# Every product of a transformer trunk layer in plain fp32 on four 32-column tiles, in place of three fp32r products of high and low parts

## The chip, the cores and the metric

The kernel runs on one core of a Trainium2 chip. The metric is the device time of one execution in microseconds, as the median of several runs. TensorE multiplies: a stationary operand of up to 128 columns is loaded into its array and a moving operand of up to 512 columns is streamed past it, into PSUM. VectorE (DVE) and ScalarE (ACT) work on SBUF and PSUM, GpSimd (POOL) does little here, and SyncE (SP) issues nearly all DMAs.

## The reference, cut to what matters

One layer of a diffusion backbone, applied to 128 context tokens and 256 latent tokens (384 together), with model width 2048. All inputs and outputs are fp32.

```python
h = rms_norm(x, n1) * (1 + sc1) + sh1
q, k, v, u = project_in(h, w_in, q_g, k_g)             # 2048 -> 4096
attn = attend(q, k, v)                                 # 16 heads of 64
na, fn = attn @ w_na_proj, fourier_mix(u) @ w_fnet_proj      # 1024 -> 2048 each
g_na, g_fn = split(sigmoid(h @ w_gate))                # 2048 -> 4096
x = x + g1 * ((g_na * na + g_fn * fn) @ w_o)           # 2048 -> 2048
h2 = rms_norm(x, n2) * (1 + sc2) + sh2
a, g = split(h2 @ w_gate_up)                           # 2048 -> 11264
x = x + g2 * ((silu(g) * a) @ w_down)                  # 5632 -> 2048
```

The six shifts, scales and gates come from two conditioning vectors through `w_mod` (2048 to 12288).

## The kernel before, in words

**A product.** TensorE takes operands of a type fp32r, a rounded fp32. To keep the precision of fp32 the kernel writes each operand as a high part H (rounded to fp32r) and a low part L (the rest, rounded too), and adds three products, H·H, H·L and L·H, into the same PSUM bank. `split` (L154 to L156) makes the parts: ScalarE casts to H, VectorE subtracts. `mm3` (L158 to L161) issues the three matmuls, one line each, so L159, L160 and L161 are most of TensorE's records.

**Weights.** `units` (L183 to L195) lists all weight blocks in the order of use, two k-tiles of 128 rows by 512 columns each, 512 KB. `load_unit` (L197) loads one on SP's queue into a `raw` tile, of which there are four. `split_unit` (L209) makes `wh` and `wl` from it, three of each. `next_unit` (L222) is called by each product loop: it splits the next unit, runs the side work that is due, asks for one more load, and returns the unit that was split one call earlier. In nearly all loops the stationary operand is 128 tokens of the activations, three token tiles per k-tile, and the weights are the moving operand, 512 columns wide.

**Activations.** `new_h` gives a k-tile's `hH` and `hL`, 384 tokens wide. They are made where the activations are: in `modulate` (L522), `mixed` (L1126), `normed` (L1305) and `split_act` (L1346).

**Stages in order of time.** The opening loads the tokens, sums the first shift and scale columns (`mod_sums`, L401), and multiplies the first k-tile (L646 on). The input projection goes over four groups of k-tiles while the rest of the columns is prepared (to about 345 us). The gate projection runs to about 660 us with the Fourier branch and attention as side work on all engines (`fourier` L762, `attention_pair` L908). Then come the two branch projections, `w_o`, and the feed-forward part from about 930 us to the end. In its first two blocks of columns (`by_features`, L1437) the weights stand and 386 columns move, the activations not yet normed with two columns for the shifts.

**Products that are plain fp32 already.** `mod_sums` (L413) and `mod_rows` (L351) multiply fp32 operands with 32 standing columns, at four column positions of the array (`tile_position=(0, q)`, q = 0, 32, 64, 96), each position with a moving operand of its own. Transposes (L429, L488, L506, L922, L925, L1018, L1242, L1302) also move fp32 operands.

**The order of work.** It is written out by hand: generators (`Paced`) are ticked once or twice a unit, and engines run their instructions in the order of issue. `rows_and_columns` (L666) sums the remaining four modulation rows on VectorE (L342) as side work up to about 1610 us.

The line that the change replaces everywhere:

```python
nc.tensor.matmul(out, aH, bH, start=start, stop=False)
nc.tensor.matmul(out, aH, bL, start=False, stop=False)
nc.tensor.matmul(out, aL, bH, start=False, stop=stop)
```

Of the kernel before, what the change touches and what calls it, by code (L numbers as in the profile page):

```python
# [14 lines left out]
F32R = mybir.dt.float32r  # L15
# [20 lines left out]
HALF = NL + NC  # L36

# [31 lines left out]


def fr(ap):

    return ap.bitcast(F32)
# [46 lines left out]
def trunk_kernel(ctx: ExitStack, tc: tile.TileContext, io: dict):  # L120
# [32 lines left out]

    def split(H, L, x):  # L154
        nc.scalar.copy(H, x)  # L155
        nc.vector.tensor_sub(L, x, fr(H))  # L156

    def mm3(out, aH, aL, bH, bL, start, stop):  # L158
        nc.tensor.matmul(out, aH, bH, start=start, stop=False)  # L159
        nc.tensor.matmul(out, aH, bL, start=False, stop=False)  # L160
        nc.tensor.matmul(out, aL, bH, start=False, stop=stop)  # L161
# [44 lines left out]
    ready = deque()  # L206
    front, behind = [], []

    def split_unit():  # L209
        if loads.got:  # L210
            _, raw = loads.take()
            H = wpool.tile([P, 2, CH], F32R, tag="wh", name=nm("wh"))
            L = wpool.tile([P, 2, CH], F32R, tag="wl", name=nm("wl"))
            n = raw.shape[1]
            split(H[:, :n], L[:, :n], raw)
            ready.append((H, L))
# [26 lines left out]
    hH = [None] * KT  # L243
    hL = [None] * KT
# [34 lines left out]
    with ExitStack() as ph:  # L279
# [164 lines left out]
        with ExitStack() as pha:  # L444
# [23 lines left out]
            loads = Ahead(load_unit, units, 2)  # L468
# [53 lines left out]
            def modulate(kt):  # L522
# [3 lines left out]
                H, L = new_h(kt)  # L526
                f = tmp.tile([P, TOK], F32, tag="hf", name=nm("hf"))
                for c, sl in ((0, slice(0, CTX)), (1, slice(CTX, TOK))):
                    sc, sh = (m[0][:, kt, c : c + 1] for m in (msc, msh))
                    nc.scalar.activation(out=f[:, sl], in_=v[:, sl], func=AF.Identity, scale=sc, bias=sh)  # L530
                split(H, L, f)
# [48 lines left out]
            h0H, h0L = new_h(0)  # L580
            f0 = tmp.tile([P, TOK], F32, tag="hf", name="hf0")

            conds2 = ((0, slice(0, CTX)), (1, slice(CTX, TOK)))

            def opening_high():
                for c, sl in conds2:
                    nc.vector.tensor_scalar(
                        h0H[:, sl], xT[0][:, 0, sl], msc[0][:, 0, c : c + 1], msh[0][:, 0, c : c + 1],
                        op0=ALU.mult, op1=ALU.add,
                    )  # L590

            def opening_low():
                for c, sl in conds2:
                    nc.scalar.activation(
                        out=f0[:, sl], in_=xT[0][:, 0, sl], func=AF.Identity,
                        scale=msc[0][:, 0, c : c + 1], bias=msh[0][:, 0, c : c + 1],
                    )
                    nc.vector.tensor_sub(h0L[:, sl], f0[:, sl], fr(h0H[:, sl]))

            opened = {}  # L600

            def open_pair(i, j):

                if j == 0:
                    _, raw = loads.take()
                    opened[i] = (
                        raw,
                        wpool.tile([P, 2, CH], F32R, tag="wh", name=nm("wh")),
                        wpool.tile([P, 2, CH], F32R, tag="wl", name=nm("wl")),
                    )  # L610
                raw, H, L = opened[i]
                split(H[:, j], L[:, j], raw[:, j])
                if j:
                    loads.more()

            opening_high()
            open_pair(0, 0)
            opening_low()
            open_pair(0, 1)
            acc = {ci: c6([P, NT, CH], "acc") for ci in ORDER}  # L620

            def beside(block):
# [7 lines left out]
                (1, 1, lambda: open_pair(1, 0)),  # L630
                (3, 1, lambda: open_pair(1, 1)),
                (7, 1, lambda: open_pair(2, 0)),
                (9, 1, lambda: open_pair(2, 1)),
                (10, 1, scales.step),
                (11, 1, scales.step),
                (13, 1, lambda: open_pair(3, 0)),
                (15, 1, lambda: open_pair(3, 1)),
                (20, 1, split_unit),
                (20, 1, loads.more),
# [6 lines left out]
            for b, (i, t) in enumerate((i, t) for i in range(8) for t in range(NT)):  # L646
                ts = [slice(n * P, (n + 1) * P) for n in range(NT)]
                _, wH, wL = opened[i // 2]
                w, l = wH[:, i % 2], wL[:, i % 2]
                if b == 0:  # L650
                    po = [mm_tile() for _ in ts]
                    for o, sl in zip(po, ts):
                        nc.tensor.matmul(o, h0H[:, sl], w, start=True, stop=False)
                    for o, sl in zip(po, ts):
                        nc.tensor.matmul(o, h0H[:, sl], l, start=False, stop=False)
                    for o, sl in zip(po, ts):
                        nc.tensor.matmul(o, h0L[:, sl], w, start=False, stop=True)
                elif i:
                    po[t] = mm_tile()
                    mm3(po[t], h0H[:, ts[t]], h0L[:, ts[t]], w, l, True, True)  # L660
                settle(ORDER[i], t, po[t], b % 2 == 0)
                beside(b)

# [60 lines left out]
            for gi, (k0, n) in list(enumerate(GROUPS))[1:]:  # L724
# [5 lines left out]
                for rate, ci in zip(CHUNKS, ORDER):  # L730
# [3 lines left out]
                    for u in range(k0, k0 + n, 2):  # L734
                        wH, wL = next_unit()
                        while prepared[0] < min(u + 2, k0 + n):
                            prep.step()
                        for t in range(NT):
                            sl = slice(t * P, (t + 1) * P)
                            for kk in range(min(k0 + n - u, 2)):  # L740
                                mm3(
                                    po[t], hH[u + kk][:, sl], hL[u + kk][:, sl], wH[:, kk], wL[:, kk],
                                    u + kk == k0, u + kk == k0 + n - 1,
                                )
# [13 lines left out]
        fHs, fLs = (fo.tile([P, 8, TOK], F32R, tag=n, name=n) for n in ("fH", "fL"))  # L758
        fH, fL = ([f[:, i] for i in range(8)] for f in (fHs, fLs))
        aT = [None] * 8  # L760

        def fourier():  # L762
            with ExitStack() as st:
# [3 lines left out]
                def table(shape, src):  # L767
                    raw = fw.tile(shape, F32, tag="fraw", bufs=2, name=nm("fraw"))
# [3 lines left out]
                def split_table(name, raw):  # L772
                    H, L = (fc.tile(raw.shape, F32R, tag=name + x, name=nm(name + x)) for x in "HL")
                    split(H, L, raw)
                    return H, L

                def load_u(g):
                    return table([P, NT, FG], s_qkvu[6 + g // 2][:, :, (g % 2) * FG : (g % 2 + 1) * FG])
# [3 lines left out]
                sums = [  # L782
                    [fw.tile([P, 2, 2, HALF], F32R, tag=f"A{x}{cc}", name=f"A{x}{cc}") for x in "HL"]
                    for cc in range(2)
                ]

                def positions(gi, cc):
                    s = slice(cc * P, (cc + 1) * P)
                    AH, AL = sums[cc]
                    o = at_tile()  # L790
                    for t in range(2):
                        mm3(
                            o[:, : 2 * NL], uH[:, 1 + t, s], uL[:, 1 + t, s], latH[:, t], latL[:, t],
                            t == 0, t == 1,
                        )
                    o2 = at_tile()
                    mm3(o2[:, :256], uH[:, 0, s], uL[:, 0, s], ctxH, ctxL, True, True)
                    for sl, src in (
                        (slice(0, NL), o[:, : 2 * NL]), (slice(NL, HALF), o2[:, : 2 * NC]),
                    ):  # L800
                        split(AH[:, :, gi, sl], AL[:, :, gi, sl], src.rearrange("p (s n) -> p s n", s=2))

                def channels(pair, cp):

                    parts = []
                    for sn in range(2):
                        w = slice(sn * FG + cp * P, sn * FG + (cp + 1) * P)
                        o = at_tile()
                        for cc in range(2):
                            AH, AL = sums[cc]  # L810
                            mm3(
                                o[:, : 2 * HALF].rearrange("p (g n) -> p g n", g=2),
                                chH[:, cc, w], chL[:, cc, w], AH[:, sn], AL[:, sn], cc == 0, cc == 1,
# [5 lines left out]
                    f = fw.tile([P, 2, TOK], F32, tag="f", name=nm("f"))  # L819
# [4 lines left out]
                    i = slice(4 * pair + cp, 4 * pair + cp + 3, 2)  # L824
                    split(fHs[:, i], fLs[:, i], f)
# [3 lines left out]
                lat = table([P, 2, 2 * NL], io["dft_lat"])  # L829
                ctx_ = table([P, 256], io["dft_ctx"])  # L830
                for _ in range(10):
                    yield
                latH, latL = split_table("lat", lat)
                ctxH, ctxL = split_table("ctx", ctx_)
                u = load_u(0)
                chan = table([P, 2, 512], io["dft_chan"])
# [756 lines left out]
```

## Time and profile before

| | |
|---|---|
| median of 3 runs | 2023.78 us (2022.6 to 2026.68) |
| the profiled execution | 2025.61 us, its span 2023.8 us |
| granted TensorE clock | 0.999 |
| TensorE matmuls (PE) | 2001.2 us busy, 99% of the span, 9488 records |
| weight loads into the array (PEld) | 1637.5 us, 81% |
| VectorE (DVE) | 1280.4 us, 63% |
| ScalarE (ACT) | 731.4 us, 36% |
| DMA | 408.62 MB, mean 202 GB/s |

A record of a matmul has a measured start; its end is modelled, and matmuls overlap in the pipeline, so a duration is longer than the time that one matmul takes from the next. What one costs is read from starts and from counts in a window. "PE" is the matmul, "PEld" the load of its stationary operand. In a row of groups stand the line, the engine, the operation, the tiles (output, then the moving and the standing operand), the shapes, the count, then busy us, the mean duration in ns, and the idle time before it with its releaser.

### The profile page before, as it was taken

How to read it: one execution, taken by the hardware profiler on the slowest of the kernel's cores; microseconds unless marked ns; L12 is line 12 of the kernel's file. 1: busy time of each engine (PE TensorE's matmuls, PEld its weight loads, DVE VectorE, ACT ScalarE, POOL GpSimd, SP SyncE). 2: the span in 40 equal slices, each digit the busy share in tenths (PEclk: the TensorE clock that was granted, in tenths of full speed). 3: DMA queues.
4: the chain of work that ended last, by engine and by line, in shares of the span. 5: the costliest groups of instructions: out<-in, count | busy, mean ns of one | idle time of the engine just before them, and what ended most of it. 6: DMA issues, size and time to landing. Idle time of an engine off the chain costs nothing.

```text
span 2023.8 us, 24499 instructions
## 1 busy us (share of the span) xinstructions
PE 2001.2 (99%) x9488; PEld 1637.5 (81%) x9488; DVE 1280.4 (63%) x1585; ACT 731.4 (36%) x1076; POOL 39.2 (2%) x82
## 2 busy tenths in 40 slices
PE   8999999999999999999999999999999999999999
PEld 5767888887878788879988888888888888888887
DVE  5745998788997887675845454455555433443753
ACT  6323332455554443334523323322232233222321
POOL 0000000000000000000000000000000000000000
PEclk9999999999999999999999999999999999999999
DMA  9896878576765697763355455546554544455553
GB/s 335 295 342 203 303 254 320 178 248 218 232 221 163 244 318 251 250 221 117 123 172 182 158 179 173 177 146 197 162 184 154 157 143 147 132 160 153 170 187 104
DMA packets 133093, 408.62 MB, mean 202 GB/s; under 512 B 15920, under 2 KB 36208, under 8 KB 132976
## 3 DMA queue, kind: packets, MB, share of 16 engines
q1 hardware_dynamic: 127200, 400.55, 60.2%
q10 hardware_dynamic: 3600, 6.34, 0.8%
q8 instruction: 74, 1.21, 0.2%
q0 software_dynamic: 2176, 0.17, 0.1%
q14 instruction: 43, 0.35, 0.1%
HBM read 379.15 MB, written 27.85 MB: 201 GB/s over the span
## 4 chain that ended last, share of the span: by engine, by line
PE 87%; DVE 7%; ACT 2%; issue 1%; DMA 1%; ACTq 0%; SPq 0%; DVEq 0%
PE mm L159 18%; PE mm L160 17%; PE mm L161 17%; PE at L160 11%; PE at L161 11%; PE at L159 11%; DVE accr L342 2%; DVE wl L156 2%; PE at L413 1%; ACT wh L155 1%; DMA wm<-in_w_mod 1%; ACT sc L994 1%; DVE pt L156 1%; PE at L351 0%; ACTq L1097 0%
## 5 line engine op out<-in xcount | busy, mean ns | idle before, releaser
L156 DVE TENSOR_TENSOR wl<-wraw,wh 128x1024 fp32r<-128x1024 f32 (+1 forms) x464 | 555.6, 1203 | 466.6 <-ACT wh L155 465.8
L155 ACT CAST wh<-wraw 128x1024 fp32r<-128x1024 f32 (+1 forms) x464 | 478.7, 1036 | 849.3 <-PE mm L161 523.8
L159 PE MATMUL mm<-wh,hH 128*128 128x512 f32 x1341 | 529.1, 395 | 0.3 <-ACT hH L155 0.3
L160 PE MATMUL mm<-wl,hH 128*128 128x512 f32 x1341 | 522.7, 390 | 1.2 <-DVE wl L156 1.2
L161 PE MATMUL mm<-wh,hL 128*128 128x512 f32 x1341 | 522.8, 390 | 0.0
L159 PEld LDWEIGHTS mm<-wh,hH 128*128 128x128 f32 x1341 | 251.9, 188 | 67.6 <-issue 12.6
L342 DVE SCALAR_TENSOR_TENSOR accr<-wmr,csz,accr 128x1024 f32<-128x1024 f32 x240 | 303.9, 1281 | 0.1
L161 PEld LDWEIGHTS mm<-wh,hL 128*128 128x128 f32 x1341 | 251.8, 188 | 53.8 <-DVE hL L156 0.6
L160 PEld LDWEIGHTS mm<-wl,hH 128*128 128x128 f32 x1341 | 252.1, 188 | 52.0 <-DVE wl L156 2.0
L160 PE MATMUL at<-wl,hH 128*128 128x512 f32 x624 | 243.1, 390 | 0.6 <-DVE wl L156 0.6
L159 PE MATMUL at<-wh,hH 128*128 128x512 f32 x624 | 243.1, 390 | 0.0
L161 PE MATMUL at<-wh,hL 128*128 128x512 f32 x624 | 242.9, 389 | 0.0
L160 PEld LDWEIGHTS at<-wl,hH 128*128 128x128 f32 x624 | 117.2, 188 | 25.8 <-DVE wl L156 1.6
L159 PEld LDWEIGHTS at<-wh,hH 128*128 128x128 f32 x624 | 117.1, 188 | 24.3
L161 PEld LDWEIGHTS at<-wh,hL 128*128 128x128 f32 x624 | 117.1, 188 | 24.2
L159 PE MATMUL mm<-wh,cH 128*128 128x512 f32 x280 | 109.1, 390 | 0.0
L161 PE MATMUL mm<-wh,cL 128*128 128x512 f32 x280 | 109.0, 389 | 0.0
L160 PE MATMUL mm<-wl,cH 128*128 128x512 f32 x280 | 109.0, 389 | 0.0
L159 PE MATMUL at<-wh,cH 128*128 128x512 f32 x200 | 77.8, 389 | 0.0
L160 PE MATMUL at<-wl,cH 128*128 128x512 f32 x200 | 77.8, 389 | 0.0
L161 PE MATMUL at<-wh,cL 128*128 128x512 f32 x200 | 77.8, 389 | 0.0
L747 DVE TENSOR_TENSOR acc<-acc,mm 128x512 f32<-128x512 f32 x60 | 40.4, 686 | 39.8 <-PE mm L161 39.7
(272 smaller groups left out, 1853.1 us busy)
## 6 DMA issues: line engine op xcount, KB each, us to landing
wraw<-in_w_gate_up SPq DMA_DIRECT2D x176, 512.0 KB, 3.8
wmr<-in_w_rows SPq DMA_DIRECT2D x128, 512.0 KB, 4.8
wraw<-in_w_down SPq DMA_DIRECT2D x88, 512.0 KB, 3.7
wraw<-in_w_gate SPq DMA_DIRECT2D x64, 512.0 KB, 4.3
wraw<-in_w_in SPq DMA_DIRECT2D x60, 512.0 KB, 5.2
wm<-in_w_mod SPq DMA_DIRECT2D x24, 768.0 KB, 6.3
wraw<-in_w_o SPq DMA_DIRECT2D x32, 512.0 KB, 4.8
wm<-in_w_mod SPq DMA_DIRECT2D x28, 512.0 KB, 6.4
```

The costliest lines, as they stand in the source:

```text
L155: nc.scalar.copy(H, x)
L156: nc.vector.tensor_sub(L, x, fr(H))
L159: nc.tensor.matmul(out, aH, bH, start=start, stop=False)
L160: nc.tensor.matmul(out, aH, bL, start=False, stop=False)
L161: nc.tensor.matmul(out, aL, bH, start=False, stop=stop)
L342: nc.vector.scalar_tensor_tensor(out=acc[:, cnd], in0=wm, scalar=sc, in1=acc[:, cnd], op0=ALU.mult, op1=ALU.add)
L413: nc.tensor.matmul(pm[q : q + 32, :w], csz[:, k, :], wm[:, kk + par, ty, :], start=k < 2, stop=k >= KT - 2, tile_position=(0, q), skip_gro ...
L747: nc.vector.tensor_add(a, a, po[t])
L994: nc.scalar.activation(out=sc[:, j, sl], in_=sc[:, j, sl], func=AF.Exp, bias=mx[:, i : i + 1], accum_out=sm[:, i : i + 1],)
```

## The change

There is no fp32r any more, and no H and L parts. A new helper `mm` takes the place of `mm3`: it cuts the standing operand into pieces of 32 columns and issues one plain fp32 matmul for each, at four column positions of the array, into four groups of 32 PSUM partitions, all with the same moving operand. In the attention scores the contraction is over 64 rows, and two heads stand at row positions 0 and 64. In the attention values each head has 64 standing columns, so two heads fill the four positions. All splits go; the products read the raw weights and one fp32 tile per activation. The freed space holds ten raw weight tiles, and loads run eight units ahead. Where a split also moved data from PSUM or changed its layout, one copy is left, on ScalarE or VectorE. The rows of `mod_sums`, `mod_rows` and the transposes stay as they are.

```diff
-    def split(H, L, x):
-        nc.scalar.copy(H, x)
-        nc.vector.tensor_sub(L, x, fr(H))
-
-    def mm3(out, aH, aL, bH, bL, start, stop):
-        nc.tensor.matmul(out, aH, bH, start=start, stop=False)
-        nc.tensor.matmul(out, aH, bL, start=False, stop=False)
-        nc.tensor.matmul(out, aL, bH, start=False, stop=stop)
+    def mm(out, a, b, start, stop, row=0, col=0):
+
+        m = a.shape[1]
+        for j in range(0, m, min(W, m)):
+            c = slice(j, j + min(W, m))
+            nc.tensor.matmul(
+                out[c], a[:, c], b, start=start, stop=stop, tile_position=(row, col + j), skip_group_check=True,
+            )
...
-        raw = wpool.tile([P, 2, CH], F32, tag="raw", bufs=4, name=nm("wraw"))
+        raw = wpool.tile([P, 2, CH], F32, tag="raw", bufs=AHEAD + 2, name=nm("wraw"))
...
-        split_unit()
         for p in front + behind:
             p.tick()
         loads.more()
-        return ready.popleft()
+        return loads.take()[1]
...
-        hH[kt] = hpool.tile([P, TOK], F32R, tag=f"tH{kt}", name=nm(f"hH{kt}_"))
-        hL[kt] = hpool.tile([P, TOK], F32R, tag=f"tL{kt}", name=nm(f"hL{kt}_"))
-        return hH[kt], hL[kt]
+        h[kt] = hpool.tile([P, TOK], F32, tag=f"t{kt}", name=nm(f"h{kt}_"))
+        return h[kt]
...
+                if i % 2 == 0 and t == 0:
+                    raw = loads.take()[1]
+                    loads.more()
+                    loads.more()
+                o = mm_tile()
+                mm(o, h[0][:, t * P : (t + 1) * P], raw[:, i % 2], True, True)
+                settle(ORDER[i], t, o, b % 2 == 0)
                 beside(b)
+            while len(loads.got) < AHEAD:
+                loads.more()
...
                 def products(cols, q, k):
-                    for i, (qx, kx) in enumerate(((qH, kH), (qH, kL), (qL, kH))):
-                        for j in range(2):
-                            nc.tensor.matmul(
-                                po[j][:, cols], qx[rows[j], q], kx[rows[j], k], start=i == 0, stop=i == 2,
-                                tile_position=(j * HD, 0),
-                            )
+                    for j in range(2):
+                        mm(po[j][:, cols], t["q"][rows[j], q], t["k"][rows[j], k], True, True, row=j * HD)
...
-                        mm3(po[t], hH[k][:, sl], hL[k][:, sl], wH[:, kk], wL[:, kk], k == 0, k == KT - 1)
+                        mm(po[t], h[k][:, sl], w[:, kk], k == 0, k == KT - 1)
```

Here `W = 32` and `AHEAD = 8`. The same replacement stands in all product loops.

More of the change, by code (lines that the diff above doesn't have):

```diff
@@ L204, in load_unit @@
         return raw[:, :n]
-    ready = deque()
     front, behind = [], []
[L209 to L216, printed above, removed]
     def mid_unit():
@@ L467, in trunk_kernel @@
                 src.more()
-            loads = Ahead(load_unit, units, 2)
+            loads = Ahead(load_unit, units, 3)
             warm_silu = small.tile([P, 1], F32, tag="warm", bufs=1, name="warm_silu")
@@ L578, in trunk_kernel @@
             prep = Paced(prepare())
[L580 to L589, printed above, removed]
-                    )
[L592 to L619, printed above, removed]
+            new_h(0)
+            for c, sl in ((0, slice(0, CTX)), (1, slice(CTX, TOK))):
+                nc.vector.tensor_scalar(
+                    h[0][:, sl], xT[0][:, 0, sl], msc[0][:, 0, c : c + 1], msh[0][:, 0, c : c + 1],
+                    op0=ALU.mult, op1=ALU.add,
+                )
             acc = {ci: c6([P, NT, CH], "acc") for ci in ORDER}
@@ L757, in trunk_kernel @@
         gst = ph.enter_context(tc.tile_pool(name="gst", bufs=4))
-        fHs, fLs = (fo.tile([P, 8, TOK], F32R, tag=n, name=n) for n in ("fH", "fL"))
-        fH, fL = ([f[:, i] for i in range(8)] for f in (fHs, fLs))
+        fs = fo.tile([P, 8, TOK], F32, tag="fs", name="fs")
         aT = [None] * 8
@@ L800, in positions @@
                     ):
-                        split(AH[:, :, gi, sl], AL[:, :, gi, sl], src.rearrange("p (s n) -> p s n", s=2))
+                        nc.scalar.copy(sums[cc][:, :, gi, sl], src.rearrange("p (s n) -> p s n", s=2))
                 def channels(pair, cp):
@@ L818, in channels @@
                     nc.scalar.copy(so, odd)
-                    f = fw.tile([P, 2, TOK], F32, tag="f", name=nm("f"))
+                    i = slice(4 * pair + cp, 4 * pair + cp + 3, 2)
+                    f = fs[:, i]
                     nc.vector.tensor_add(f[:, :, CTX : CTX + NL], even[:, :, :NL], so[:, :, :NL])
@@ new lines, in keys_first @@
+                    (nc.vector.tensor_copy if b0 % 8 else nc.scalar.copy)(
+                        t["pt"][:, dst], o[:, : len(some) * P].rearrange("p (b q) -> p b q", q=P)
+                    )
+            def values():
+                pt = t["pt"]
+                po = at_tile()
+                for kc in range(3):
+                    for j in range(2):
+                        s = slice(j * HD, (j + 1) * HD)
+                        mm(
+                            po[s, CTX:TOK].rearrange("p (t q) -> p t q", t=2), vp[:, kc + 1, s],
+                            pt.rearrange("p (t b) q -> p t b q", t=2)[:, :, 2 * kc + j],
+                            kc == 0, kc == 2, col=j * HD,
+                        )
+                for j in range(2):
+                    s = slice(j * HD, (j + 1) * HD)
+                    mm(po[s, :CTX], vp[:, 0, s], pt[:, 6 + j], True, True, col=j * HD)
+                nc.scalar.copy(aT[hp], po[:, :TOK])
@@ L1161, in trunk_kernel @@
             gl = [None, None]
-            for i, bH, bL in ((1, fH, fL), (0, aH, aL)):
+            for i, b in ((1, [fs[:, k] for k in range(8)]), (0, aT)):
                 _, gl[i] = gates.take()
@@ L1212, in trunk_kernel, with shifts @@
     xhp = phx.enter_context(tc.tile_pool(name="xhp", bufs=1))
-    xw = [xhp.tile([P, 12, XW], F32R, tag=f"x{n}", name=f"x{n}") for n in "HL"]
-    xv = []
-    def wide(kt):
-        return [x[:, kt] for x in xw] if kt < 12 else [x[:, kt - 12] for x in xv]
-    def shifts(some, k0):
-        H, L = some
-        c = slice(k0, k0 + H.shape[1])
-        nc.scalar.copy(H[:, :, TOK:], msh[1][:, c])
-        nc.vector.tensor_sub(L[:, :, TOK:], msh[1][:, c], fr(H[:, :, TOK:]))
+    xw = xhp.tile([P, KT, XW], F32, tag="xw", name="xw")
+    def shifts():
+        nc.scalar.copy(xw[:, :, TOK:], msh[1])
     pho = ctx.enter_context(ExitStack())
@@ L1286, in trunk_kernel @@
     xvp = phx.enter_context(tc.tile_pool(name="xvp", bufs=1))
-    xv += [xvp.tile([P, 4, XW], F32R, tag=f"v{n}", name=f"v{n}") for n in "HL"]
     rB = xvp.tile([P, TOK], F32, tag="rB", name="rB")
-    shifts(xv, 12)
     def inverse():
@@ L1308, in normed @@
         conds = ((0, slice(0, CTX)), (1, slice(CTX, TOK)))
-        for step in range(KT + 2):
+        for step in range(KT + 1):
             kt = step
             if kt < KT:
-                xH, xL = (fr(x[:, :TOK]) for x in wide(kt))
-                v = vs[:, kt % 4]
-                nc.vector.tensor_add(v, xH, xL)
-                nc.vector.tensor_mul(v, v, rB)
+                nc.vector.tensor_mul(vs[:, kt % 4], xw[:, kt, :TOK], rB)
             kt = step - 1
@@ L1342, in act_tiles, with keep_act, turn_act @@
             return [new_h(f) for f in range(4)]
[L1343 to L1351 removed]
+        c = actp.tile([P, 4, TOK], F32, tag=f"c{c4}", name=nm("c"))
+        return [c[:, f] for f in range(4)]
+    def keep_act(c4, src, cs):
+        for f, c in enumerate(act_tiles(c4)):
+            cs.append(c)
+            (nc.vector.tensor_copy if f % 2 else nc.scalar.copy)(
+                c.rearrange("p (t i r) -> p t i r", t=NT, r=32) if len(src.shape) > 3 else c, src[:, f]
+            )
             yield
[L1354 removed]
+    def turn_act(c4, tr, cs):
         nc.sync.dma_start(s_turn, tr.rearrange("p g k t r -> p g (k t r)"))
@@ L1365, in turn_act @@
         yield
-        yield from split_act(c4, raw.rearrange("p i f t r -> p f t i r"), cH, cL)
+        yield from keep_act(c4, raw.rearrange("p i f t r -> p f t i r"), cs)
     def late_norm(o, sg, half):
@@ L1404, in trunk_kernel @@
     final = len(FF_PARTS) - 1
-    parts = [([], []) for _ in FF_PARTS]
+    parts = [[] for _ in FF_PARTS]
     def by_tokens(half):
@@ L1432, in by_tokens @@
         if not half:
[L1433 removed]
+            work = Paced(turn_act(c4, tr, cs), 1, 1)
             work.step()
@@ L1449, in by_features @@
                     k = u + kk
-                    xH, xL = wide(k)
-                    mm3(po[f][:, : xH.shape[1]], wH[:, kk, s], wL[:, kk, s], xH, xL, k == 0, k == KT - 1)
+                    mm(po[f][:, :XW], w[:, kk, s], xw[:, k], k == 0, k == KT - 1)
                 if u < KT - 2:
@@ L1483, in trunk_kernel @@
     for part, c4, half in ff_jobs():
-        cH, cL = parts[part]
+        cs = parts[part]
         if c4 is None:
```

227 lines of the change are left out of this document (53 added, 174 removed).

## The prediction

> **What bounds the kernel now.** I read the page first: busy shares, then the chain that ended last.
>
> ```profile
> span 2023.8 us, 24499 instructions
> ...
> PE 2001.2 (99%) x9488; PEld 1637.5 (81%) x9488; DVE 1280.4 (63%) x1585; ACT 731.4 (36%) x1076; POOL 39.2 (2%) x82
> ...
> PE 87%; DVE 7%; ACT 2%; issue 1%; DMA 1%; ACTq 0%; SPq 0%; DVEq 0%
> ```
>
> TensorE is the bound in nearly every microsecond, and VectorE and ScalarE are not. A busy PE could still be a pipeline with slack, since ends are modelled, so I went on to the count of matmuls in a long window of the feed-forward part, with the clock granted in full (the columns are the window, its length, PE's busy time and count, clock, DMA share, GB/s).
>
> ```profile
> 1310.00:1510.00 200.00, 200.00 (x885) 1.00 0.56 175
> ```
>
> A matmul starts 200 / 885 = 226 ns after the one before it, and an fp32 product, three of them, takes 678 ns. The count of products is the count of one of `mm3`'s lines over the whole span.
>
> ```profile
> 0.00:2023.80 2023.80, 1089.88 (x2805) 526.87 (x2805) 1.00 0.61 202
> ```
>
> That row is L159. By the code 2640 products move 512 columns (w_in 384, gate 384, branches 192, w_o 192, gate-up 960, down 528), 128 move 386, and 40 are Fourier's: 2808, and three more of the 512 stand at L653, so all are there. The 2640 take 2640 x 0.678 = 1790 us of the 2024. The question is therefore one price: what does a plain fp32 product cost on four tiles side by side?
>
> **The price of the new product.** The kernel already runs such matmuls, in the sums of the modulation. These are groups with 32 standing columns (count, busy us, mean ns), and below them one group of fp32r and one of fp32 transposes over 128 standing columns.
>
> ```profile
> L413 PE MATMUL at<-wm,csz 128*32 128x384 f32 x192 | 17.6, 491 | 0.0
> L413 PE MATMUL at<-wm,csz 128*32 128x256 f32 x192 | 13.7, 387 | 0.7 <-DMA wm<-in_w_mod 0.7
> L351 PE MATMUL at<-accr,ones 128*32 128x512 f32 x64 | 9.6, 605 | 1.7 <-ACT sc L976 1.0 <-DVE accr L342 0.7
> ...
> L413 PE MATMUL at<-wm,csz 128*32 128x128 f32 x64 | 2.6, 278 | 2.0 <-DMA wm<-in_w_mod 2.0
> ```
>
> ```profile
> L160 PE MATMUL mm<-wl,hH 128*128 128x512 f32 x1341 | 522.7, 390 | 1.2 <-DVE wl L156 1.2
> ...
> L1018 PE MATMUL at<-ident,sc 128*128 128x128 f32 x112 | 15.7, 276 | 1.7 <-DVE sc L1004 1.6
> ```
>
> Two things are to be seen. First the counts: L351 is written four times in each of eight sums, 32 matmuls, and there are 64 records; L413 is written 224 times and there are 448. A plain fp32 matmul becomes two passes. Second the length: from 128 to 384 moving columns the duration grows by (491 - 278) / 256 = 0.832 ns a column. The transposes, one fp32 pass over the whole array, take as long at 128 columns (276) as the small tiles do (278), so the slope belongs to fp32 and not to four tiles being in each other's way. At 512 columns the fp32 pass has 605 against 390 for fp32r, which is 215 ns more.
>
> Durations are modelled, so I checked starts: one sum at L351, eight records, in three short windows (PE's count is of records that touch the window).
>
> ```profile
> 261.36:261.40 0.04, 0.03 (x4) 0.03 (x5) 1.00 1.30 525
> 261.40:261.82 0.42, 0.42 (x4) 0.13 (x8) 1.00 1.14 409
> 261.82:261.85 0.03, 0.03 (x8) 0.00 (x0) 1.00 0.66 273
> ```
>
> ```profile
> 261.37 1.07 PE L351 MATMUL at<-accr,ones 128*32 128x512 f32 x8
> ...
> 262.37 0.50 PE L159 MATMUL mm<-wh,hH 128*128 128x512 f32 x1
> ...
> 262.50 0.59 ACT L355 COPY accr<-at 128x512 f32<-128x512 f32 x1 [4.48 <-PE at L351]
> ```
>
> Four start within 40 ns, none starts for 0.42 us, then the other four start. So the tiles do run side by side, and each spends one pass price before its next pass. ScalarE's copy, which needs all eight, starts at 262.50, as the ends say.
>
> The pass price at 512 columns lies between 0.832 x 512 = 426 ns (the slope alone) and 455 ns (the start distance above, which has the first weight load in it: these four loads run just ahead of their matmuls, the next four well before theirs). In a long stream every load has a whole pass to hide in, so I take 430, near the slope. A product is two passes: **860 ns against 678**. Four tiles of 32 columns make one product of 128 columns; concurrency only fills the array again.
>
> **The change part by part.** Sums are against the profiled span, 2023.8 us.
>
> - The 2640 products: 2640 x 0.860 = 2270 us instead of 1790: **+480**. Bounds 2249 to 2402, so +459 to +612.
> - The 128 products with 386 columns. Now three starts, 178 ns apart (first and last of twelve records, 1.96 us / 11):
>
> ```profile
> 970.02 0.33 PE L159 MATMUL mm<-xH,wh 128*128 128x386 f32 x1
> ...
> 971.98 0.34 PE L161 MATMUL mm<-xH,wl 128*128 128x386 f32 x1
> ```
>
>   128 x 3 x 0.178 = 68 us; then 128 x 2 x 0.430 x 386/512 = 83: **+15**. Fourier's 40 products are no wider, so at most 40 x 3 x 0.178 = 21 us now, and with the same ratio **+4**.
> - Attention. Scores of a pair of heads go from 455.22 to 456.80, values from 461.02 to 462.90:
>
> ```profile
> 455.22 0.44 PE L955 MATMUL at<-kH,qH 64*128 64x384 f32 x2
> ...
> 456.80 0.50 PE L159 MATMUL mm<-wh,hH 128*128 128x512 f32 x1
> ...
> 461.02 0.33 PE L1036 MATMUL at<-pt,v 128*128 128x128 f32 x2
> 461.19 0.93 PE L1039 MATMUL at<-pt,v 128*128 128x256 f32 x6
> 461.96 0.34 PE L1036 MATMUL at<-pt,v 128*128 128x128 f32 x2
> ...
> 462.90 0.40 PE L159 MATMUL mm<-wh,hH 128*128 128x512 f32 x1
> ```
>
>   Scores move 384, 384 and 128 columns with both heads side by side, before and after: 2 x 0.84 x 896 = 1.51 us against 1.58, nothing. Values put both heads side by side too: 2 x 0.84 x (3 x 256 + 128) = 1.51 against 1.88, and eight pairs give **-3**.
> - The splits on VectorE and ScalarE go. They lie beside the products, so their work itself is worth nothing; what counts is when PE waited. Such stalls are few:
>
> ```profile
> 0.00:20.43 20.43, 11.77 (x116) 8.59 (x116) 11.02 (x26) 13.59 (x35) 0.69 (x6) 1.00 0.92 339
> ...
> 2014.00:2023.80 9.80, 5.12 (x23) 3.92 (x21) 4.04 (x6) 0.00 (x0) 0.00 (x0) 0.87 0.20 80
> ```
>
> ```profile
> PE mm L160 <- DVE wl L156: 2.5, 3, 1.3
> ```
>
>   PE idles 2023.8 - 2001.2 = 22.6 us, 8.7 of it in the opening's first 20.4 us and 4.7 at the very end, which stay. That leaves 9.2 us, of waits for low parts (as in the last row) and for chains of the side work: **-7**, as an estimate (0 to -9). In the opening the first product no longer waits for a second copy of its activations:
>
> ```profile
> 20.46 1.14 PE L653 MATMUL mm<-wh,hH 128*128 128x512 f32 x3 [1.12 <-ACT hf L594]
> ```
>
>   **-1**. At those places the next to be late is whatever the slower PE waits for, and since each unit takes 27% longer, every chain and load has more time.
> - Shape changes of the array. In the rows of L351 the next fp32r matmul comes 1.00 us after the first of eight and is 0.11 longer than others (0.50 for 0.39), where two passes stream 0.86: 0.14 to 0.25 us a group. There are 60 such groups (384 / 8 = 48 wide ones of L413, 64 / 16 = 4 narrow ones, 8 of L351); they lose their change, and some 50 groups of transposes and scores gain one. I take 0, with 12 us either way.
> - Loads. The queue of SP now holds back behind raw tiles that wait for splits; ten tiles end that. Five more units, 2.6 MB, go out in the opening ahead of the column weights, about 7.7 us at the 339 GB/s above, while the opening's 24 products take 24 x 0.18 = 4.4 us longer. With column weights four tiles ahead I take 0, at worst +3.
>
> Sum: 480 + 15 + 4 - 3 - 7 - 1 = +488, a span of **2512 us**. The profiled execution took 2025.61, 1.8 over its span, and the median of the runs is 2023.78, so 2512 stands for the median too; I say 2510.
>
> **The rivals.**
>
> *Weight loads show.* Eight loads a product instead of three, and if each pass pays the 25 ns that the first four paid at L351, a pass is 455 ns: +612 + 8, 2644 us. Against it, the second four loads were done by 261.82 in the rows above, where the window counts no load at all.
>
> *The stream feeds too slowly.* A product is 16 instructions in 860 ns, 54 ns each. The densest regular stream of short matmuls above is L1039: six with their loads from 461.19 to 461.96, 64 ns an instruction, though those also stream 256 columns. If 64 were the feed, a product takes 1.02 us, 2640 x (1.02 - 0.86) = 422 us on top of 2512: 2934. Against it: four matmuls and five loads started within 40 ns at 261.36.
>
> *The tiles don't run side by side, so the change doesn't do what it says.* If the two passes of one piece stand next to each other and starts keep program order, the second pass waits for its own tile, and the next tile starts only with it: four pass prices a product, 1.72 us, 2640 x 0.86 = 2270 us on top: 4782. In the row at 261.40 to 261.82 this is not what happened: four firsts started before any second. By the Trainium skill, page "TensorE: Matmul & The Clock Gate", section "Part 3: Packing small matmuls — row/col tiling", matmuls keep strict program order in start and end. By that rule the trace agrees only if the passes are already sorted, four firsts and then four seconds, in what TensorE is given.
>
> *Not slower.* At L351 and L413 four different operands move. In the change all four tiles move the same one. If the fp32 slope came from four operands sharing a read path, one shared operand would stream at the fp32r slope, 605 - 390 = 215 ns less than 430: 215 ns a pass, 430 a product, 2640 x (0.430 - 0.678) = -655, about 1345 us with the narrow products. It decides from a pass under some 0.678 / 2 = 339 ns. Against it stand the transposes, one operand at a time and the same 276 ns.
>
> **How the numbers follow.** Forecast 0.80, loads that show 0.08, feed 0.05, no concurrency 0.03, not slower 0.04. What a measurement of this kernel can tell from no change is about 0.2%, 4 us. The forecast's own bounds are 2512 - 21 - 2 - 12 = 2477 and, for passes a little above 430, some 2560; the range takes in loads that show and the margins for shape changes: 2470 to 2655. Faster 0.035, same 0.005, slower 0.96.
>
> **What would show it.** Right: 21,120 matmuls of 512 columns, about 8 x 200 / 0.86 = 1860 in a 200 us window; starts in fours, 430 ns apart; VectorE far under its 1280 us; PE full. The slope is wrong if starts in fours come 215 ns apart; feed, if a tile's matmuls start evenly spread; program order, if never more than two run together; and the loads, if a pass is 455. A PE with gaps while SP's raw loads land late would put the error in the sum's last lines.

## The result and the profile after

The changed kernel takes **2495.62 us** (median of 4 runs, 2495.24 to 2497.26) against 2023.62 us of the kernel before on the same chip: a ratio of 1.2331, with a 95% interval of 1.231 to 1.2352. It is slower by 23%. The forecast was 2510 us in a range of 2470 to 2655.

The page of the changed kernel: busy shares and the chain that ended last.

```profile
span 2493.6 us, 51427 instructions
...
PE 2478.7 (99%) x23896; PEld 885.1 (35%) x23896; DVE 651.5 (26%) x901; ACT 215.0 (9%) x505; POOL 39.5 (2%) x82
...
PE 99%; DMA 1%; SPq 0%; DVE 0%; ACT 0%; issue 0%; ACTq 0%
```

VectorE does half of what it did and ScalarE less than a third, and next to none of that is in the time, because TensorE sets it from beginning to end. What TensorE does is seen in the groups of the one line that now issues every product (tiles, shapes, count, busy us, mean ns).

```profile
L155 PE MATMUL mm<-wraw,h 128*32 128x512 f32 x10752 | 1194.1, 593 | 1.0 <-DVE h L563 1.0
L155 PE MATMUL at<-wraw,h 128*32 128x512 f32 x4992 | 559.9, 592 | 0.0
L155 PE MATMUL mm<-wraw,c 128*32 128x512 f32 x2240 | 251.3, 592 | 0.0
L155 PE MATMUL at<-wraw,c 128*32 128x512 f32 x1600 | 182.2, 592 | 0.0
L155 PE MATMUL mm<-wraw,fs 128*32 128x512 f32 x576 | 63.6, 592 | 0.0
L155 PE MATMUL at<-wraw,aT 128*32 128x512 f32 x512 | 57.5, 592 | 0.0
L155 PE MATMUL at<-xw,wraw 128*32 128x386 f32 x512 | 44.8, 488 | 0.0
...
L155 PE MATMUL mm<-wraw,aT 128*32 128x512 f32 x256 | 29.7, 592 | 0.0
L155 PE MATMUL at<-wraw,fs 128*32 128x512 f32 x192 | 22.1, 592 | 0.0
```

The counts at 512 columns add up to 21,120, eight for each of 2640 products: four pieces, two passes each. Their mean, 592 or 593 ns, is that of L351 before (605) without the 25 ns that the first four of its eight records take longer. The price itself is read from counts and starts. First a long window, the same as was shown of before, then five short ones in the steady stream (PE's count is of records that touch the window).

```profile
1310.00:1510.00 200.00, 200.00 (x1869) 75.34 (x1865) 24.67 (x24) 11.53 (x20) 0.00 (x0) 1.00 0.44 134
```

```profile
1500.12:1500.18 0.06, 0.06 (x8) 1.00 0.49 137
1500.18:1500.55 0.37, 0.37 (x8) 1.00 0.87 343
1500.55:1500.61 0.06, 0.06 (x8) 1.00 0.82 341
1500.61:1500.98 0.37, 0.37 (x8) 1.00 0.92 376
1500.98:1501.04 0.06, 0.06 (x8) 1.00 1.17 478
```

In each long stretch the same eight run, four draining and four streaming; four start within 60 ns, and again 0.43 us later. Taking off the five or so of the 1869 that only reach into the window, 200 us hold 1864, so eight take 0.858 us. That is a product. Before, with the two or so taken off its 885 in the same way, the starts stand 226.67 ns apart and a product takes 0.680 us, 2 ns more than the 0.678 of the prediction.

### The profile page after: what moved, and what is told of

The parts are those of the page before. It is cut to its first block, busy times and chain, and to the rows that moved or that the text cites. A ratio compares the mean times of both kernels' runs of the same rounds, so it can differ in the third digit from the quotient of the medians.

```text
span 2493.6 us, 51427 instructions
## 1 busy us (share of the span) xinstructions
PE 2478.7 (99%) x23896; PEld 885.1 (35%) x23896; DVE 651.5 (26%) x901; ACT 215.0 (9%) x505; POOL 39.5 (2%) x82
## 4 chain that ended last, share of the span: by engine, by line
PE 99%; DMA 1%; SPq 0%; DVE 0%; ACT 0%; issue 0%; ACTq 0%
PE mm L155 61%; PE at L155 35%; PE at L396 1%; DMA wm<-in_w_mod 1%; PE at L908 1%; PE at L334 0%; DMA xc<-in_x_in 0%; PE at L1103 0%; PE at L412 0%; SPq L444 0%; PE at L828 0%; PE at L831 0%; PE mm L1103 0%; ACT mrow L404 0%; DVE d L1321 0%
## 5 line engine op out<-in xcount | busy, mean ns | idle before, releaser
L155 PE MATMUL mm<-wraw,h 128*32 128x512 f32 x10752 | 1194.1, 593 | 1.0 <-DVE h L563 1.0
L155 PEld LDWEIGHTS mm<-wraw,h 128*32 128x32 f32 x10752 | 381.4, 110 | 744.9 <-issue 722.3
L155 PE MATMUL at<-wraw,h 128*32 128x512 f32 x4992 | 559.9, 592 | 0.0
L155 PEld LDWEIGHTS at<-wraw,h 128*32 128x32 f32 x4992 | 190.6, 110 | 343.7 <-issue 340.6
L155 PE MATMUL mm<-wraw,c 128*32 128x512 f32 x2240 | 251.3, 592 | 0.0
L155 PE MATMUL at<-wraw,c 128*32 128x512 f32 x1600 | 182.2, 592 | 0.0
L155 PEld LDWEIGHTS mm<-wraw,c 128*32 128x32 f32 x2240 | 90.5, 110 | 149.8 <-issue 147.9
L155 PEld LDWEIGHTS at<-wraw,c 128*32 128x32 f32 x1600 | 64.7, 110 | 107.0 <-issue 106.2
L155 PE MATMUL mm<-wraw,fs 128*32 128x512 f32 x576 | 63.6, 592 | 0.0
L155 PE MATMUL at<-wraw,aT 128*32 128x512 f32 x512 | 57.5, 592 | 0.0
```

What stands on the lines that cost most here:

```text
L155: nc.tensor.matmul(out[c], a[:, c], b, start=start, stop=stop, tile_position=(row, col + j), skip_group_check=True,)
```

## The experiments

### How many pieces: one of 128 columns, two of 64

The first kernel has 128 here, the second 64.

```diff
-W = 32
+W = 128
```

> The changed kernel with pieces of 128 standing columns instead of 32 (W = 128): one plain fp32 matmul over the whole array a product, nothing else changed. Theory (the price is two fp32 passes of 429 ns each at 512 columns, and four tiles only fill the array again): the same two passes a product, so 2490 to 2530 us, the upper part if part of a weight load of 128 columns shows, as 13 ns of it may in each fp32r matmul of the kernel before. Rival (four operand streams share a read path and slow each other): one stream alone takes 215 ns a pass and the time falls to about 1350 us. Rival (the tiles themselves bring speed beyond filling the array): well over 2600 us.

> The changed kernel with pieces of 64 standing columns (W = 64), two tiles side by side. Theory: starts come in twos, 429 ns apart, 2490 to 2515 us. Shared read path: between the whole array and four tiles, 1350 to 2490 us. If the width of a piece mattered through its weight load alone, the time lies between that of 32 and that of 128 columns.

Measured: 2499.6 us (2497.76 to 2501.01) with the whole array, ratio to before 1.2347, interval 1.2327 to 1.2368; and 2503.06 us (2502.16 to 2504.17) with two pieces, 1.2368, interval 1.2349 to 1.2386. One window of each, the whole array first:

```profile
1710.00:1910.00 200.00, 200.00 (x468) 1.00 0.47 142
```

```profile
1710.00:1910.00 200.00, 200.00 (x934) 1.00 0.46 141
```

Both times lie in the ranges of the theory. The counts are a quarter and a half of 1869. A pass over 128 standing columns comes every 200 / 466 = 429 ns with one operand streaming and no neighbour. So the price belongs to the plain fp32 pass. It has nothing to do with four streams sharing a path, which was the rival on the other side, and the width of the piece does not matter to it. The larger weight load of 128 columns is hidden in a pass of that length.

The few microseconds between the three kernels have another order than the pieces have: 2495.6 with 32, 2499.6 with 128, 2503.1 with 64. The sums of the modulation stand on 32 columns and the transposes on 128, so with 32 the transposes differ from the products' shape, with 128 the sums (and the attention values, which are 64 wide there), with 64 both. The traces show what such a change of shape costs. Below are the last products ahead of a sum, the sum, and the first products behind it, with 32 columns and then with 128; then the same for eight transposes.

```profile
304.70 0.61 PE L155 MATMUL at<-wraw,h 128*32 128x512 f32 x4
305.13 1.04 PE L334 MATMUL at<-accr,ones 128*32 128x512 f32 x8
305.99 0.61 PE L155 MATMUL mm<-wraw,h 128*32 128x512 f32 x4
```

```profile
312.31 0.59 PE L155 MATMUL at<-wraw,h 128*128 128x512 f32 x1
312.83 1.07 PE L334 MATMUL at<-accr,ones 128*32 128x512 f32 x8
313.83 0.70 PE L155 MATMUL mm<-wraw,h 128*128 128x512 f32 x1
```

```profile
659.30 0.61 PE L155 MATMUL mm<-wraw,h 128*32 128x512 f32 x4
659.85 1.09 PE L908 MATMUL at<-ident,sc 128*128 128x128 f32 x8
660.87 0.64 PE L155 MATMUL mm<-wraw,h 128*32 128x512 f32 x4
```

```profile
667.01 0.59 PE L155 MATMUL mm<-wraw,h 128*128 128x512 f32 x1
667.44 1.04 PE L908 MATMUL at<-ident,sc 128*128 128x128 f32 x8
668.32 1.02 PE L155 MATMUL mm<-wraw,h 128*128 128x512 f32 x2
```

From product to product a sum takes 1.29 us where it has the products' shape and 1.52 where it has not, and the transposes 1.57 where they differ and 1.31 where they don't. So a place where the shape changes and changes back costs about a quarter of a microsecond. By the starts, the sums stand in 31 places between products, so 31 x 0.24 = 7.4 us is what the kernel with 64 columns has over that with 32. The transposes stand in some 30, which nearly evens it out between 32 and 128. The values then add 8 x 0.27 = 2.1 us with 128, and some 2 of the 4 us stay open.

### Few tiles of raw weights

```diff
-AHEAD = 8
+AHEAD = 2
...
-            loads = Ahead(load_unit, units, 3)
+            loads = Ahead(load_unit, units, 2)
...
                     raw = loads.take()[1]
                     loads.more()
-                    loads.more()
```

> The changed kernel with four raw weight tiles instead of ten and loads two units ahead instead of eight (AHEAD = 2, two loads at the start, one a unit in the opening). Theory (TensorE is the bound and a unit of six products takes 5.1 us, a load lands in about 4): the same within 5 us of 2495.6. Rival (the ten tiles keep TensorE fed, and part of what the change saved in stalls is theirs): 2505 to 2560 us, with waits of PE for the raw weights.

Measured: 2496.36 us (2494.18 to 2498.22), ratio 1.2334, interval 1.2315 to 1.2352, no different from the changed kernel and as its theory had it. The ten tiles bring nothing here; two units ahead already cover a load.

### The order in which pieces are issued

The changed kernel goes around the four positions product by product. Three kernels issue more for one position before the next, in the feed-forward blocks by tokens and the down projection (1488 products).

```diff
+    def mm_by_tile(args):
+
+        for j in range(0, P, W):
+            c = slice(j, j + W)
+            for out, a, b, start, stop in args:
+                nc.tensor.matmul(
+                    out[c], a[:, c], b, start=start, stop=stop, tile_position=(0, j), skip_group_check=True,
+                )
...
-                for kk in range(2):
-                    k = u + kk
-                    mm(po[t], h[k][:, sl], w[:, kk], k == 0, k == KT - 1)
+                mm_by_tile([(po[t], h[k][:, sl], w[:, k - u], k == 0, k == KT - 1) for k in (u, u + 1)])
```

That is two products, four passes, a position. The second takes all six products of a unit, twelve passes; the third the three token tiles of one k-tile, six passes.

> The changed kernel with another order of issue in the feed-forward blocks by tokens and the down projection: for each token tile both k-tiles' products of one 32-column piece are issued before the next piece, so four passes for one column position stand together, then four for the next. 1488 of the 2640 products are reordered, nothing is left out. Theory A (matmuls start in the order of issue, and the four firsts then four seconds at the summing of the modulation rows come from an order sorted by pass): the last pass of a piece runs beside the first of the next, three of four passes alone, 12 x 429 + 429 ns or so for two products instead of 1716, about +3.4 us for each of 744 pairs, near 5000 us. Theory B (each column position takes its own next matmul out of a window of waiting instructions): no loss, 2490 to 2500 us. In between, if the window is short: 2600 to 4000 us.

> The changed kernel, and in the feed-forward blocks by tokens and the down projection all six products of a unit are issued piece by piece: twelve passes for one column position, then twelve for the next, 24 instructions with their loads. Nothing is left out. With four passes for one position together nothing was lost. Theory A (any number of waiting instructions can be passed over): 2490 to 2500 us. Theory B (a window of waiting instructions, as long as a few tens): three positions ahead are 72 instructions away, so fewer than four run together: 1488 products at up to 1.3 to 2 times 858 ns, 2900 to 3700 us.

> The changed kernel; in the feed-forward blocks by tokens and the down projection the three products of one k-tile are issued piece by piece, six passes for one column position and then six for the next. Nothing is left out. With four passes together nothing was lost; with twelve, a piece started in every ninth pass of the one before (2502.82, then 2506.29, 8 x 429 + 30 ns), so when four of its passes were left. Theory A (matmuls enter in the order of issue, and each column position holds about four): a piece starts every 6 - 4 = 2 passes, three run together, a product takes 8 x 429 / 3 = 1144 ns instead of 858, 1488 x 0.286 = +426, 2920 us. Theory B (one shared window of some 16 to 24 instructions, whatever the position): a piece of 12 instructions starts when the last of the one before enters the window, near full speed, 2495 to 2600 us.

Measured (medians of 2 runs each): **2495.25 us** with four passes a position, **4655.74 us** with twelve (2.3002 times before, interval 2.296 to 2.3044), and **2984.73 us** with six (1.4742, interval 1.4712 to 1.4771). With four, program order had near 5000 us and failed. With twelve both ranges failed, 2490 to 2500 and 2900 to 3700 us. With six the rule made from the first two runs came near. A window of each, in that order:

```profile
1710.00:1910.00 200.00, 200.00 (x1871) 90.64 (x1867) 32.98 (x37) 5.43 (x10) 0.00 (x0) 1.00 0.47 141
```

```profile
2500.00:2700.00 200.00, 200.00 (x694) 55.97 (x691) 13.64 (x15) 2.72 (x5) 0.00 (x0) 1.00 0.19 56
```

```profile
2000.00:2200.00 200.00, 200.00 (x1354) 69.71 (x1350) 29.21 (x34) 2.50 (x5) 0.00 (x0) 1.00 0.32 95
```

With twelve, short windows at the starts of successive passes show how far two pieces overlap.

```profile
2502.80:2502.84 0.04, 0.04 (x3) 0.02 (x2) 0.00 (x0) 0.00 (x0) 0.00 (x0) 1.00 0.00 0
...
2504.10:2504.15 0.05, 0.05 (x4) 0.01 (x1) 0.00 (x0) 0.00 (x0) 0.00 (x0) 1.00 0.21 82
2504.55:2504.60 0.05, 0.05 (x3) 0.03 (x1) 0.00 (x0) 0.00 (x0) 0.00 (x0) 1.00 0.20 82
2504.98:2505.03 0.05, 0.05 (x2) 0.03 (x1) 0.00 (x0) 0.00 (x0) 0.00 (x0) 1.00 0.00 0
2505.41:2505.46 0.05, 0.05 (x2) 0.04 (x1) 0.00 (x0) 0.00 (x0) 0.00 (x0) 1.00 0.00 0
```

At 2502.80 a new piece's first pass starts beside the old piece's, at 2504.10 both still run with one pass each just ended, and from 2504.98 one piece runs alone. The new piece starts when four passes of the old one are left. The overlap is four passes of twelve, which repeats every 8 passes and gives 12 x 4 pieces in 4 x 8 x 0.43 us for six products, 2.3 us a product: 1488 x (2.3 - 0.858) = +2146, measured +2160. With the same rule six passes a position overlap four deep too, a new piece in every second pass, three running. The expectation from it, 2920, was 65 us short: 44 ns a product, or 33 ns for each of the four pieces of three products. With twelve passes the starts of pieces stand 3.46 us apart, again some 30 ns over 8 x 429. This is near the 25 ns that the first pass at L351 takes longer, so it may be a weight load that shows; no run tells. The rival of one shared window falls, since it had 2495 to 2600.

One rule fits the three runs: matmuls enter in the order of issue, each column position holds about four, running or waiting, and when one is full it holds up the others; up to there each position runs on its own. Five passes were not tried. By the Trainium skill, page "TensorE: Matmul & The Clock Gate", section "Part 3: Packing small matmuls — row/col tiling", matmuls start and end strictly in program order. By that rule, only the last of four passes would run beside the next piece, so two products would take 13 passes, 2.8 us each, more than the 2.3 us that twelve took; the run with four, at 0.858, disagrees with it, and the measurement decides. No stream here shows whether the two passes of one piece stand next to each other in what TensorE is given.

### What the splits cost before

Two kernels take the waits and then the work out of the kernel before. In both, from the input projection's second group on, all products read one pair of weight parts made once.

The first goes on splitting each unit, into tiles that nothing reads (two of each); the second splits only the first unit. Neither computes the layer any more: the products leave out their own weights.

```diff
+            if not fixed:
+                fixed.extend(wpool.tile([P, 2, CH], F32R, tag=t, bufs=1, name=nm(t)) for t in ("fwh", "fwl"))
+                split(*fixed, raw)
...
             split(H[:, :n], L[:, :n], raw)
-            ready.append((H, L))
+            ready.append(fixed)
```

```diff
-            H = wpool.tile([P, 2, CH], F32R, tag="wh", name=nm("wh"))
-            L = wpool.tile([P, 2, CH], F32R, tag="wl", name=nm("wl"))
-            n = raw.shape[1]
-            split(H[:, :n], L[:, :n], raw)
-            ready.append((H, L))
+            if not fixed:
+                fixed.extend(wpool.tile([P, 2, CH], F32R, tag=t, bufs=1, name=nm(t)) for t in ("fwh", "fwl"))
+                split(*fixed, raw)
+            ready.append(fixed)
```

> The kernel before, with fp32r and three products, but from the input projection's second group on every product reads one fixed pair of weight parts made once; each unit is still loaded and still split, on both engines, into tiles that nothing reads. Left out: the dependence of the products on their own weights. It prices the waits for weight parts alone. Theory (the prediction's idle count of 9 us was too small because PE's modelled busy time hides late starts; in the starts of the L159 to L161 records some 28 us lie above 226 ns a matmul, 11 of them ahead of L160): 2008 to 2016 us. Rival (those late starts are not waits for weight parts but shape changes and side work): 2019 to 2024 us.

> As the run with the fixed pair of weight parts, but without the splits: the units are loaded and nothing reads them. Left out: the splits of the weights (some 445 on each of VectorE and ScalarE) and the products' dependence on their own weights. Theory: TensorE stays the bound, and what is gained above the fixed pair is what free engines do for the side work's chains in the attention stage: 3 to 8 us less than that run, 2003 to 2012 us. Rival (the split work itself costs TensorE time, through memory ports for example): 226 ns a matmul falls toward 216 and the time to about 1930 us.

Measured against 2024.65 us: 2022.49 us without the waits (ratio 0.9989, interval 0.9979 to 0.9998), and 2011.11 us without the work (0.9936, interval 0.9922 to 0.9949). The first expectation failed: what it called waits for weight parts is worth 2 us, not 11, so its rival holds. The second had the time right, 2003 to 2012 us, but gave the work alone 3 to 8 us where it brought 11, and its rival fell. The waits of PE in the kernel before, and then in the first of the two:

```profile
PE at L1018 <- DVE sc L1004: 1.6, 3, 0.6
...
PE at L375 <- DVE pt L156: 1.0, 1, 1.0
...
PE mm L159 <- ACT hH L155: 0.3, 1, 0.3
```

```profile
PE at L1022 <- DVE sc L1008: 2.3, 3, 1.7
PE mm L159 <- ACT hH L155: 1.3, 2, 0.9
...
PE at L379 <- DVE pt L156: 1.0, 1, 1.0
```

With VectorE still as busy, TensorE goes on waiting for the softmax and for other parts, some of it longer than before. Without the work, only the one for `hH` is left of these three, and the time falls by 11 us more.

```profile
PE mm L159 <- ACT hH L155: 0.3, 1, 0.3
```

The starts of the matmuls say how much that is in the profiled executions. The transposes of the attention stage come 5.4 us late in all in the kernel before, 5.3 us where the splits go on, and not at all without them. The stretches of products gain 6.2 us when they no longer wait for their parts and 5.0 without the work, and without the work the sums and the opening gain 3 us as well. The waits alone bring 5 us between the profiled executions, where the medians give 2: that run's times go from 2019.2 to 2024.8 us, and the profiled one, 2020.2, is among the lower.

The 226 ns of a matmul didn't move; the count in the same window as before is 884 against 885, and the starts stand 226.67 ns apart in both:

```profile
1310.00:1510.00 200.00, 200.00 (x884) 165.75 (x883) 46.65 (x54) 7.10 (x14) 0.00 (x0) 1.00 0.48 176
```

So the splits cost the kernel before some 13.5 us, a part in the waits of the products and more by holding up the side work on the same engines. A shared port that slows the matmuls does not show.

### The split work put back into the changed kernel

```diff
+            nc.scalar.copy(H[:, :n], raw)
+            nc.vector.tensor_sub(L[:, :n], raw, H[:, :n].bitcast(F32))
```

> The changed kernel with the split work of each weight unit put back on ScalarE and VectorE, into tiles that nothing reads (two of each), and loads four units ahead instead of eight. No product waits for it except through the side work that shares the engines. Theory (the split work cost the kernel before some 11 us by delaying the side work's chains; with units of 5.1 us instead of 4.1 there is more room): 2497 to 2503 us, so part of what it cost there. Rival (what the splits cost came from waits of the products alone): 2494 to 2497 us, as without the work.

Measured: 2497.83 us (2497.6 to 2498.24), ratio 1.2337, interval 1.2317 to 1.2358. This is 2.2 us above the changed kernel and at the low edge of what the theory had. All four times lie above the changed kernel's four, but the intervals of the ratios overlap, so it tells at most that the work costs little once a unit lasts 5.1 us.

### Attention alone in plain fp32

```diff
-                    for i, (qx, kx) in enumerate(((qH, kH), (qH, kL), (qL, kH))):
-                        for j in range(2):
-                            nc.tensor.matmul(
-                                po[j][:, cols], qx[rows[j], q], kx[rows[j], k], start=i == 0, stop=i == 2,
-                                tile_position=(j * HD, 0),
-                            )
+                    for j in range(2):
+                        mm(po[j][:, cols], t["q"][rows[j], q], t["k"][rows[j], k], True, True, row=j * HD)
...
-                        for i, x in enumerate(pt):
-                            nc.tensor.matmul(
-                                po[j][:, CTX:TOK].rearrange("p (t q) -> p t q", t=2), w[1 + kc],
...
+                    for j in range(2):
+                        s = slice(j * HD, (j + 1) * HD)
+                        mm(
+                            po[s, CTX:TOK].rearrange("p (t q) -> p t q", t=2), vp[:, kc + 1, s],
...
```

> The kernel before, with the attention alone taken from the changed one: scores and values in plain fp32 on 32-column pieces, no parts of q, k, the probabilities and v. All other products stay as three of fp32r. Theory (values are 0.37 us a pair of heads shorter, scores even, the chains on VectorE and ScalarE shorter, and some 20 more shape changes of 0.1 to 0.25 us): 2014 to 2024 us, 2018 taken. Rival (shape changes cost more than the values bring): 2025 to 2032 us.

Measured: 2020.91 us (2019.46 to 2024.37) against 2024.65, ratio 0.9985, interval 0.9976 to 0.9994. Of the versions that leave nothing out it is the only one faster than both kernels, by 0.15%. The theory's range holds, but the trace gives another reason than the one it put first.

```profile
452.38 1.79 PE L169 MATMUL at<-k,q 64*32 64x384 f32 x48
454.10 0.50 PE L160 MATMUL mm<-wh,hH 128*128 128x512 f32 x1
```

```profile
458.45 1.72 PE L169 MATMUL at<-pt,vp 128*32 128x256 f32 x32
460.10 0.50 PE L160 MATMUL mm<-wh,hH 128*128 128x512 f32 x1
```

Values take 1.65 us a pair of heads where they took 1.88, because two heads share the four positions. Scores take 1.72 where they took 1.58. With the change of shape ahead of them counted, eight pairs gain 1.2 us in the values and lose 1.1 in the scores. The transposes of the attention stage, late by 5.4 us before, are on time here. That is nearly all of the 6.1 us between the two profiled executions; the medians differ by 3.7. By these traces plain fp32 pays here because it takes the splits of the attention off VectorE and ScalarE, and hardly by its matmuls; no run took the two apart.

## Why the prediction was right

- **The price, 860 ns against 678.** Measured 858 against 680. It carried the forecast, and it could be read before the change because the kernel already ran 512 such passes. The run over the whole array shows the reason given for it, that the slope belongs to fp32 and that four pieces only fill the array again. The transposes were weak evidence for that: they stand at one width, which gives no slope, and an fp32r matmul of that width already took 253 ns against their 276.

```profile
L1036 PE MATMUL at<-pt,v 128*128 128x128 f32 x32 | 5.5, 253 | 0.0
```

- **The 128 products at 386 columns, +15.** Their passes now last 488 ns on average, 105 less than at 512, or 0.83 ns a column as the slope had it. By the starts they went from 68.4 to 83.7 us, +15.3. Attention's matmuls, forecast at -3, came to -2 by the starts (values -3.2, scores +1.1), and Fourier's products, at +4, to +3.6.
- **The splits, -7 and -1.** This term was mis-sized. Idle time of PE gave 9 us as its upper bound, and leaving out the weight splits alone brought 13.5. PE's busy time is modelled and runs over late starts, so idle is no upper bound. The reason was wrong in part as well: it named waits for low parts first, and these are worth 2 us by the medians, 5 in the profiled executions.
- **Shape changes, 0.** Right within some 3 us, but partly by luck. The prediction counted 60 groups of sums against some 50 of transposes and scores. They stand in 31 and some 30 places between products, and the quarter of a microsecond that a place costs is gained at the sums and lost at the transposes.
- **Loads, 0, and the ten tiles.** Right: two units ahead give the same time.
- **The sum.** Between the profiled executions the span grew from 2023.8 to 2493.6 us, by 470 where the sum had 488. The pass price took 5280 x 0.8 ns, 4 us, off. The 885, which still had the records that only reach into the window, took off 5 more: 2640 x 2 ns. The splits took 5.5. Some 3 us are left for shape changes and the rest; the terms are not known to a microsecond.
- **The rivals.** Weight loads stay hidden: a pass in the stream takes 429 ns, not 455. The stream is fed in time: 16 instructions in 858 ns, and the counts with 32, 64 and 128 columns agree. The four positions run side by side, though the order of issue can undo it, as the twelve passes show. And a shared operand streams no faster.

## What to carry to other kernels

Cutting a full 128 columns into pieces brings no speed: pieces side by side pay where the standing operand has few columns, as in the sums of L351, whose four products start within 40 ns. Before a change of type, look for operations of the new type that the trace already has, and take their price from counts and starts of records, not from busy shares. When pieces are used, go around the positions with no more than four passes for one before the next. Count too how often the stream changes its shape, at a quarter of a microsecond for a change and back.

## What the runs showed of the hardware that I had not expected

- Up to four passes for one column position can stand together in the stream at no cost (2495.25 us); six cost 20% (2984.73) and twelve nearly double the time (4655.74), with 1488 of the 2640 products issued that way.
- A plain fp32 pass takes 429 ns at 512 columns whether 32, 64 or 128 columns stand, and the weight load of 128 columns is then fully hidden, while three fp32r matmuls take 226 ns each, 12 more than half of a 429 ns pass.
- Work that no product waits for can still cost TensorE time through the engines that it fills: 2 us of gain by the medians without the waits for weight parts, 13.5 without the splits. The transposes of the attention stage were as late with splits that nothing reads (5.3 us) as before (5.4).
- A stretch of another shape between products costs about 0.25 us for the change and the change back: 1.52 against 1.29 us for a sum, 1.57 against 1.31 for eight transposes.
